# Expert stage of a two-layer decoder: order of weight loads, halves of two weights, and the place of the last scatters

## The chip, the cores and the metric

The kernel runs on one NeuronCore of one Trainium2 chip. Its engines work side by side, each from an in-order queue of its own: TensorE (PE; its weight loads are shown apart as PEld), VectorE (DVE), ScalarE (ACT), GpSimd (POOL) and SyncE (SP), which issues the DMA transfers here. The metric is the device time of one execution, in microseconds; the kernel is run several times and the median counts.

## What is computed

Two layers of a decoder trunk over 256 tokens of width 1024. Each layer is a mixer (sparse and block-sparse attention in layer 0, stick-breaking attention in layer 1), a LayerNorm, a hierarchical mixture of experts (16 experts, hidden width 256), and another LayerNorm. The change lies in the mixture of experts:

```python
def hierarchical_moe(x, w_grp, b_grp, w_rt, b_rt, w_gate, w_up, w_down):
    p_grp = jax.nn.softmax((x @ w_grp + b_grp).astype(jnp.float32), axis=-1)
    g = jnp.argmax(p_grp, axis=-1)
    ...
    top_val, top_idx = lax.top_k(logits, TOPK_IN_GROUP)
    w_e = jax.nn.softmax(top_val, axis=-1) * w_g[..., None]
    expert_id = g[..., None] * EXPERTS_PER_GROUP + top_idx
    combine = jnp.sum(jax.nn.one_hot(expert_id, N_EXPERTS, dtype=jnp.float32) * w_e[..., None], axis=2)
    def per_sequence(args):
        xs, cs = args
        h = jax.nn.silu(jnp.einsum('sd,edf->sef', xs, w_gate)) * jnp.einsum('sd,edf->sef', xs, w_up)
        return jnp.einsum('sef,efd->sd', h * cs[..., None].astype(h.dtype), w_down)

for layer in range(DEPTH):
    x = layer_norm(DEEPNORM_ALPHA * x + mix, ln_mix_g[layer], ln_mix_b[layer])
    ffn = hierarchical_moe(x, ...)
    x = layer_norm(DEEPNORM_ALPHA * x + ffn, ln_ffn_g[layer], ln_ffn_b[layer])
```

Each token uses two experts, so the kernel computes only the rows that are routed, with all 16 experts' weights read once per layer.

## The kernel before

`trunk` runs mixer, expert stage, mixer, expert stage. The expert stage (`moe_`, L1040 to L1453) treats the experts in seven **units** (`POS`, L1030): units 0 to 3 are pairs of experts with 64 slots each, unit 4 (`OV`) takes the tokens over an expert's slots, units 5 and 6 are four experts each with 32 slots. Experts 0 to 5 (units 0 to 2) stand at fixed places; the others are sorted by their load on the chip, so that the addresses of their weights are read from a table (`eid`, L1191) by SP.

Each unit has the same steps on PE:

- **gather** (L1231): tokens are picked into slots by products with a one-hot matrix.
- **front**, the gate and up products (L1264): over 8 chunks of the width; each expert of a unit works in a strip of the array of its own (`lanes`, `tile_position`), 2 or 4 strips at a time. One such product in the code is two rows of the trace.
- **act_h**: silu on ACT (L1270) and a product on DVE (L1272); then two transposes on PE (L1279) and a copy `hT` on ACT (L1280).
- **down** (L1296): the down products, in the same strips, for two halves of the columns; ACT and DVE split each half of the result into a high and a low part (L190, L198).
- **scatter** (L1305, in the last unit's `scatter_end` L1311): the parts are added into four accumulators (two token tiles by two column halves), 8 products of 512 columns a unit.

The steps of neighbouring units are interleaved by hand (L1375 to L1448): front(u+1) stands ahead of down(u), and so on. Within that program order a scheduler of the framework places each instruction on its engine by its own estimate of when operands are there; `tc.issue_after(ins)` forbids it to place an instruction ahead of `ins`.

Weights come through one queue, issued by SP in order. Gate and up weights (`wgu`) go into a ring of six 2 MB buffers (`wtile`, tag `w`), which the mixer's weights share; down weights (`wd`, 1 MB) into four buffers of their own (`wd_tile`), one extra (`wd_extra`) and one place of the ring. A load can be issued once PE has read the last of what stood in its buffer, and a load that waits holds up all behind it on SP. Units 0 and 1 are loaded by `load_gu` (L427): one tile holds chunks 0 to 3 of both experts, the next chunks 4 to 7. Unit 2 is loaded at L1052 to L1058 by whole experts, each in one tile, so that both tiles are read until the end of front(2). Units 5 and 6 are loaded by quarters (`load_gu_of`, L1194): chunks 2j and 2j+1 of four experts, four transfers of 512 KB. In the text wd(2,1) is the down weight of unit 2's second expert, and down(5), front(2) a unit's step.

At the end of the stage `out_tile` adds the residual and does the LayerNorm: between the layers `mid` (L1529), which also transposes the result into `xT` (L309, copies L316 on ACT) for the next mixer's first projection (L254); at the end of the program `fin` (L1559).

Of the kernel before, what the change touches and what calls it, by code (L numbers as in the profile page):

```python
# [17 lines left out]
S, D, NT, NCH = 256, 1024, 2, 8  # L18
# [15 lines left out]
def trunk(ctx, tc, io):  # L34
# [10 lines left out]
    last = {}  # L45
# [23 lines left out]
    def chunks(w):  # L69
        return w.rearrange("p (c n) -> p c n", c=NCH)  # L70
# [969 lines left out]
    def moe_(pm, wk, l, x, lg, xhl, out_tile, before_end):  # L1040
# [9 lines left out]

        wloads[l, 2, 0] = {}
        for i in range(2):  # L1052
            w = chunks(wtile("wgu"))
            SP.dma_start(w, io["wgu"][l * NE + 4 + i])
            for c in range(NCH):
                wloads[l, 2, 0][i, c] = w[:, c]
            if i == 0:
                load_d_at(2, 0, wd_extra())  # L1058
# [155 lines left out]


# [43 lines left out]
        def gate_up(u, g):  # L1259
            ws = wloads[l, u, 0]  # L1260
            pg = pmt()
            for c in range(NCH):
                for k, r in lanes(u):
                    PE.matmul(pg[r, :], g[:, c, BASE[u] + r.start:BASE[u] + r.stop], ws[k, c],  # L1264
                              start=(c == 0), stop=(c == NCH - 1), tile_position=(0, r.start))
            return pg
# [23 lines left out]
        def down(u, dst=(None, None)):  # L1290
            ys, hT, wd = [], hs[u], wloads[l, u, 1]
            for h in range(2):
                y = pmt()
                for fc in range(2):
                    for k, r in lanes(u):
                        PE.matmul(y[r, :], hT[:, fc, r], wd[k][:, fc, h * 512:h * 512 + 512],  # L1296
                                  start=(fc == 0), stop=(fc == 1), tile_position=(0, r.start))
                ys.append(split_y(y, dst[h]))
            return ys
# [7 lines left out]
        def scatter_end(u1, u2):  # L1307

            for u, h, t in ((u2, 0, 0), (u1, 0, 1), (u1, 1, 1), (u2, 1, 0), (u2, 0, 1), (u2, 1, 1)):
                for i in range(2):  # L1310
                    last["PE"] = PE.matmul(oacc[t][h], ST[:, u, t * 128:t * 128 + 128], ys[u][h][i], start=False, stop=(u == u2 and i == 1)).ins  # L1311
# [77 lines left out]
        do_down(0)  # L1389
        load_d_at(2, 1, wd_tile())  # L1390
        load_d_of(3, 0, wd_tile())
        load_gu_of(5, 0)
# [43 lines left out]
        load_d_of(6, 3, wd_extra())  # L1436
# [4 lines left out]
        hid[6], _ = act_h(6, pg)  # L1441
        do_tr(6)
        act_set("natural_log_exp_and_others")
        do_scatter(5, [0])
# [3 lines left out]
        scatter_end(5, 6)  # L1448
# [204 lines left out]
```

## Time and profile before

| | |
|---|---|
| median of 3 runs | 533.94 us (533.82 to 534.5) |
| the profiled execution | 533.85 us, of which the span of instructions is 531.9 us |
| expert stage, layer 0 / layer 1 | about 163 to 271 us / 411 to 517 us |
| DMA moved | 150.02 MB, mean 282 GB/s over the span; 317 to 431 GB/s in the stretches of the expert stages |
| granted PE clock | 1.00 from 16 us to the end of the last product |

The profile is one execution. Times in its rows are microseconds from the start of the span; a row of the timeline gives start, duration, engine, line, output and inputs, how many instructions are merged in it, and in brackets the idle time of the engine before it and what ended that idle time. Line numbers are those of the kernel before.

### The profile page before, as it was taken

The page shows a single profiled execution, that of the slowest core. Times are in us where ns is not written, and L with a number is a line of the kernel's source. Part 1 is how long each engine was busy: PE and PEld are TensorE (multiplying, and loading weights), DVE is VectorE, ACT ScalarE, POOL GpSimd, SP SyncE. Part 2 cuts the span into 40 slices and gives each one's busy share as a digit, 9 for nine tenths or more (in the row PEclk, how much of TensorE's full clock was granted, in tenths as well). Part 3 has the DMA queues.
Part 4 walks back from the last instruction along what each step waited for, and adds up shares of the span by engine and source line. Part 5 has one row for each costly group of instructions (what it writes and reads, how often), then busy time and mean ns, then how long its engine had stood idle before and what let it go on. Part 6 is the DMA issues. An engine that isn't in the chain of part 4 may idle for free.

```text
span 531.9 us, 8516 instructions
## 1 busy us (share of the span) xinstructions
PE 501.4 (94%) x3201; PEld 316.4 (59%) x3201; DVE 289.5 (54%) x824; ACT 220.8 (42%) x433; POOL 7.6 (1%) x18
## 2 busy tenths in 40 slices
PE   8899989999999999999899999999999999999980
PEld 6687656676676354543354996898777454363320
DVE  5878796849669621221166555555648861141125
ACT  4545645547556121121144347556747321131022
POOL 1000000000020000000000000000002000000000
PEclk9999999999999999999999999999999999999995
DMA  8999500009938999999997980003976599999952
GB/s 243 381 429 429 217 0 1 1 0 393 412 152 322 415 363 335 421 422 422 432 430 307 370 341 1 0 1 147 427 297 238 224 394 342 402 423 419 427 217 84
DMA packets 25536, 150.02 MB, mean 282 GB/s; under 512 B 3472, under 2 KB 4112, under 8 KB 14992
## 3 DMA queue, kind: packets, MB, share of 16 engines
q1 hardware_dynamic: 25488, 149.41, 70.1%
q8 instruction: 27, 0.44, 0.3%
q14 instruction: 21, 0.17, 0.1%
HBM read 148.35 MB, written 1.05 MB: 281 GB/s over the span
## 4 chain that ended last, share of the span: by engine, by line
PE 82%; DVE 9%; ACT 4%; DMA 2%; issue 1%; SPq 0%; ACTq 0%; DVEq 0%
PE pmt L1264 16%; PE pmt L1296 9%; PE pmt L1231 4%; PE acc L1305 3%; PE acc L246 3%; PE acc L245 3%; PE acc L398 3%; PE acc L244 3%; PE acc L396 3%; PE acc L397 3%; PE acc L254 3%; DMA wb<-w 2%; PE acc L268 2%; PE acc L266 2%; PE acc L267 2%; PE z L880 2%
## 5 line engine op out<-in xcount | busy, mean ns | idle before, releaser
L1264 PE MATMUL pmt<-wgu,xg 128*64 128x512 f32 (+1 forms) x512 | 92.8, 595 | 0.0
L1264 PEld LDWEIGHTS pmt<-wgu,xg 128*64 128x64 f32 (+1 forms) x512 | 27.2, 123 | 52.9 <-issue 50.8
L190 ACT ACTIVATE wh<-wb 128x1024 fp32r<-128x1024 f32 (+2 forms) x44 | 41.1, 944 | 37.4 <-PE acc L267 19.7
L193 DVE TENSOR_TENSOR wl<-wb,wh 128x512 fp32r<-128x512 f32 (+1 forms) x72 | 45.1, 660 | 19.0 <-ACT wh L190 18.9
L1296 PE MATMUL pmt<-wd,hT 128*64 128x512 f32 (+1 forms) x256 | 53.9, 597 | 0.9 <-ACT hT L1280 0.9
L198 DVE TENSOR_TENSOR yl<-pmt,yh 128x512 fp32r<-128x512 f32 x20 | 13.8, 690 | 47.5 <-ACT yh L190 47.5
L246 PE MATMUL acc<-wl,xhl 128*128 128x512 f32 (+1 forms) x96 | 37.7, 395 | 1.5 <-DVE wl L193 1.5
L244 PE MATMUL acc<-wh,xhl 128*128 128x512 f32 (+1 forms) x96 | 37.3, 389 | 1.4 <-ACT wh L190 1.4
L245 PE MATMUL acc<-wh,xhl 128*128 128x512 f32 (+1 forms) x96 | 37.0, 386 | 0.0
L1272 DVE SCALAR_TENSOR_TENSOR hh<-pmt,cs,silu 128x256 f32<-128x256 f32 x12 | 5.8, 484 | 56.8 <-ACT silu L1270 56.8
L1270 ACT ACTIVATE silu<-pmt 128x256 f32<-128x256 f32 x12 | 4.6, 384 | 76.1 <-PE pmt L1264 76.1
L190 ACT ACTIVATE yh<-pmt 128x512 fp32r<-128x512 f32 x20 | 11.9, 597 | 55.9 <-PE pmt L1296 55.9
L1296 PEld LDWEIGHTS pmt<-wd,hT 128*64 128x64 f32 (+1 forms) x256 | 15.3, 123 | 27.0 <-issue 24.9
L1231 PEld LDWEIGHTS pmt<-Poh,xhl 128*128 128x128 f32 x192 | 24.4, 188 | 5.3 <-issue 3.2
L266 PE MATMUL acc<-xhl,wh 128*128 128x256 f32 x96 | 27.5, 287 | 0.0
L1231 PE MATMUL pmt<-Poh,xhl 128*128 128x256 f32 (+1 forms) x192 | 26.7, 292 | 0.3 <-DVE xg L1239 0.3
L268 PE MATMUL acc<-xhl,wl 128*128 128x256 f32 x96 | 26.9, 280 | 0.0
L267 PE MATMUL acc<-xhl,wh 128*128 128x256 f32 x96 | 26.8, 279 | 0.0
L398 PE MATMUL acc<-xol,oT 128*128 128x512 f32 x64 | 26.1, 412 | 0.0
L396 PE MATMUL acc<-xo,oT 128*128 128x512 f32 x64 | 25.9, 410 | 0.0
L397 PE MATMUL acc<-xo,oT 128*128 128x512 f32 x64 | 25.5, 401 | 0.0
L581 ACT ACTIVATE Pm<-pst,nm 128x128 f32<-128x128 f32 (+1 forms) x48 | 19.8, 419 | 10.7 <-DVE nm L579 9.5
(368 smaller groups left out, 984.0 us busy)
## 6 DMA issues: line engine op xcount, KB each, us to landing
wd<-wd SPq DMA_DIRECT2D x34, 1024.0 KB, 11.0
wgu<-wgu SPq DMA_DIRECT2D x64, 512.0 KB, 11.1
wgu<-wgu SPq DMA_DIRECT2D x14, 2048.0 KB, 12.1
wb<-w1s SPq DMA_DIRECT2D x6, 2048.0 KB, 19.1
wo<-wo SPq DMA_DIRECT2D x4, 2048.0 KB, 16.2
wgu<-wgu SPq DMA_DIRECT2D x8, 1024.0 KB, 7.2
wb<-w SPq DMA_DIRECT2D x3, 2048.0 KB, 22.0
wb<-w SPq DMA_DIRECT2D x2, 1024.0 KB, 8.9
```

Source lines behind the costliest of these rows:

```text
L190: A.activation(dst_h, src, AF.Copy)
L193: V.tensor_tensor(dst_l[:, i], src[:, i], dst_h[:, i].bitcast(F32), OP.subtract)
L244: PE.matmul(a[t][:, :n], xh[:, cc, ts], wh[:, c, :n], start=(cc == 0), stop=False)
L245: PE.matmul(a[t][:, :n], xl[:, cc, ts], wh[:, c, :n], start=False, stop=False)
L246: PE.matmul(a[t][:, :n], xh[:, cc, ts], wl[:, c, :n], start=False, stop=(cc == NCH - 1))
L266: PE.matmul(o, wh[:, c, fs], xh[:, cc], start=(cc == 0 and f % 2 == 0), stop=False, skip_group_check=True)
L396: PE.matmul(a[t][h], oc[:, 0, ts], wh[:, hs], start=first, stop=False)
L397: PE.matmul(a[t][h], oc[:, 1, ts], wh[:, hs], start=False, stop=False)
L398: PE.matmul(a[t][h], oc[:, 0, ts], wl[:, hs], start=False, stop=last)
L1231: PE.matmul(p[:, 0:w], src[:, t, c * 128:c * 128 + 128], P[:, t, u * 128:u * 128 + w], start=(t == 0 and src is xh), stop=(t == 1 and src ...
L1264: PE.matmul(pg[r, :], g[:, c, BASE[u] + r.start:BASE[u] + r.stop], ws[k, c], start=(c == 0), stop=(c == NCH - 1), tile_position=(0, r.start))
L1296: PE.matmul(y[r, :], hT[:, fc, r], wd[k][:, fc, h * 512:h * 512 + 512], start=(fc == 0), stop=(fc == 1), tile_position=(0, r.start))
```

## The change

It has four edits, all in the expert stage, for both layers.

1. **Pair 2 by chunk halves.** Unit 2's gate and up weights are loaded by `load_gu(l, 2)` as those of units 0 and 1 are, with wd(2,0) behind both instead of between them.
2. **Order of loads.** The first quarter of unit 5 (`load_gu_of(5, 0)`) goes ahead of wd(2,1) and wd(3,0).
3. **The last down weight**, wd(6,3), is loaded in two transfers of 512 columns each (`load_d_half`).
4. **Scatters.** The scatters of unit 5 may not be placed ahead of the last gate product of unit 6, and those of unit 6 not ahead of its last down product; `scatter_end` takes its six pairs in another order.

```diff
         load_gu(l, 1)
-
-        wloads[l, 2, 0] = {}
-        for i in range(2):
-            w = chunks(wtile("wgu"))
-            SP.dma_start(w, io["wgu"][l * NE + 4 + i])
-            for c in range(NCH):
-                wloads[l, 2, 0][i, c] = w[:, c]
-            if i == 0:
-                load_d_at(2, 0, wd_extra())
+        load_gu(l, 2)
+        load_d_at(2, 0, wd_extra())
...
+        def load_d_half(u, i, wd, h):
+
+            hs = slice(h * 512, h * 512 + 512)
+            SP.dma_start(wd[:, :, hs], io["wd"][l * NE:(l + 1) * NE][ds(expert(POS[u][i]), 1)].rearrange("e p (f n) -> p (e f) n", f=2)[:, :, hs])
+            wloads.setdefault((l, u, 1), {})[i] = wd
...
-                    PE.matmul(pg[r, :], g[:, c, BASE[u] + r.start:BASE[u] + r.stop], ws[k, c],
-                              start=(c == 0), stop=(c == NCH - 1), tile_position=(0, r.start))
+                    last["G"] = PE.matmul(pg[r, :], g[:, c, BASE[u] + r.start:BASE[u] + r.stop], ws[k, c],
+                                          start=(c == 0), stop=(c == NCH - 1), tile_position=(0, r.start)).ins
...
-        def scatter_end(u1, u2):
-
-            for u, h, t in ((u2, 0, 0), (u1, 0, 1), (u1, 1, 1), (u2, 1, 0), (u2, 0, 1), (u2, 1, 1)):
-                for i in range(2):
-                    last["PE"] = PE.matmul(oacc[t][h], ST[:, u, t * 128:t * 128 + 128], ys[u][h][i], start=False, stop=(u == u2 and i == 1)).ins
+        def scatter_end(u1, u2, down2):
+
+            for u, h, t in ((u1, 0, 1), (u1, 1, 1), (u2, 0, 0), (u2, 1, 0), (u2, 0, 1), (u2, 1, 1)):
+                with (tc.issue_after(down2) if u == u2 else nullcontext()):
+                    for i in range(2):
+                        last["PE"] = PE.matmul(oacc[t][h], ST[:, u, t * 128:t * 128 + 128], ys[u][h][i], start=False, stop=(u == u2 and i == 1)).ins
...
         do_down(0)
+        load_gu_of(5, 0)
         load_d_at(2, 1, wd_tile())
         load_d_of(3, 0, wd_tile())
-        load_gu_of(5, 0)
...
-        load_d_of(6, 3, wd_extra())
+        w63 = wd_extra()
+        for h in range(2):
+            load_d_half(6, 3, w63, h)
...
         pg = front(6)
         hid[6], _ = act_h(6, pg)
+        gate6 = last["G"]
         do_tr(6)
         act_set("natural_log_exp_and_others")
-        do_scatter(5, [0])
+        with tc.issue_after(gate6):
+            do_scatter(5, [0])
...
-        scatter_end(5, 6)
+        with tc.issue_after(gate6):
+            scatter_end(5, 6, last["D"])
```

The order of instructions on the engines changes at few places. On PE, at the end of the expert stage (layer 0's rows; layer 1's are alike), from the last down product of unit 5 on, before. `wgu_2581` and `wgu_2586` are the last two quarters of unit 6's gate and up weights, `yh` and `yl` the two parts of unit 5's result, `x8` eight products in a row:

```order
L1264 MATMUL pmt_2673<-wgu_2581,xg_2499 32x512
L1305 MATMUL acc_1878<-yh_2649,ST_1877 128x512
L1305 MATMUL acc_1878<-yl_2650,ST_1877 128x512
L1264 MATMUL pmt_2673<-wgu_2581,xg_2499 32x512
L1305 MATMUL acc_1879<-yh_2662,ST_1877 128x512
L1305 MATMUL acc_1879<-yl_2663,ST_1877 128x512
L1311 MATMUL acc_1880<-yh_2649,ST_1877 128x512
L1311 MATMUL acc_1880<-yl_2650,ST_1877 128x512
L1311 MATMUL acc_1881<-yh_2662,ST_1877 128x512
L1311 MATMUL acc_1881<-yl_2663,ST_1877 128x512
L1264 MATMUL pmt_2673<-wgu_2581,xg_2499 32x512 x6
L1264 MATMUL pmt_2673<-wgu_2586,xg_2499 32x512 x8
```

And in the changed kernel, from the same place on, where L1263, L1304 and L1278 are the lines of gate products, scatters and transposes:

```order
L1263 MATMUL pmt_2674<-wgu_2581,xg_2499 32x512 x8
L1263 MATMUL pmt_2674<-wgu_2586,xg_2499 32x512 x8
L1304 MATMUL acc_1878<-yh_2649,ST_1877 128x512
L1304 MATMUL acc_1878<-yl_2650,ST_1877 128x512
L1304 MATMUL acc_1879<-yh_2662,ST_1877 128x512
L1304 MATMUL acc_1879<-yl_2663,ST_1877 128x512
L1311 MATMUL acc_1880<-yh_2649,ST_1877 128x512
L1278 MATMUL pmt_2712<-identf_79,hh_2709 128x128 x2
L1311 MATMUL acc_1880<-yl_2650,ST_1877 128x512
L1311 MATMUL acc_1881<-yh_2662,ST_1877 128x512
L1311 MATMUL acc_1881<-yl_2663,ST_1877 128x512
```

The sixteen gate products stand together, five scatters stand between them and the transposes, and three between the transposes and unit 6's down products, which follow in both kernels in the same order. Ahead of these rows the order of PE is unchanged.

On SP, in the middle of layer 0's expert stage (layer 1's is alike), before. `wgu_2082` is the overflow unit's weight, `wgu_2134` the first quarter of unit 5, `wd_2130` and `wd_2132` are wd(2,1) and wd(3,0), and TENSOR_LOAD and ISA fetch an expert's number:

```order
L1207 DMA wgu_2082<-wgu 128x4096
L1045 DMA wd_2130<-wd 128x2048
L1212 ISA
L1212 DMA wd_2132<-wd 128x2048
L1191 TENSOR_LOAD eid_1872
L1191 ISA x2
L1200 ISA
L1200 DMA wgu_2134<-wgu 128x1024
```

In the changed kernel the four transfers of that quarter (now `wgu_2130`) follow the overflow unit's directly; the rows from the last of them on, with L1184, L1193 and L1205 for the lines L1191, L1200 and L1212 of before, and `wgu_2241` as the second quarter of unit 5:

```order
L1184 TENSOR_LOAD eid_1872
L1184 ISA x2
L1193 ISA
L1193 DMA wgu_2130<-wgu 128x1024
L1045 DMA wd_2171<-wd 128x2048
L1205 ISA
L1205 DMA wd_2173<-wd 128x2048
L1193 ISA
L1193 DMA wgu_2241<-wgu 128x1024
```

The two down weights have moved behind all of the quarter.

On ACT one instruction moves, between the layers, in the LayerNorm behind layer 0's expert stage. `lnst_2757` is the statistics tile of the first token tile, `lnst_2828` that of the second; L316 copies the first tile's transposed result. Before:

```order
L353 ACTIVATE acc_1878,lnst_2757<-xn_127,lnst_2757 128x512
L353 ACTIVATE acc_1879,lnst_2757<-xn_127,lnst_2757 128x512
L356 ACTIVATE lnst_2757<-lnst_2757 128x1
L357 ACTIVATE lnst_2757<-lnst_2757 128x1
L316 ACTIVATE xT_2756<-pmt_2806 128x4x128
L316 ACTIVATE xT_2756<-pmt_2813 128x4x128
L353 ACTIVATE acc_1880,lnst_2828<-xn_127,lnst_2828 128x512
L353 ACTIVATE acc_1881,lnst_2828<-xn_127,lnst_2828 128x512
```

In the changed kernel (the statistics tiles are 2758 and 2829 there):

```order
L353 ACTIVATE acc_1878,lnst_2758<-xn_127,lnst_2758 128x512
L353 ACTIVATE acc_1879,lnst_2758<-xn_127,lnst_2758 128x512
L356 ACTIVATE lnst_2758<-lnst_2758 128x1
L357 ACTIVATE lnst_2758<-lnst_2758 128x1
L353 ACTIVATE acc_1880,lnst_2829<-xn_127,lnst_2829 128x512
L316 ACTIVATE xT_2757<-pmt_2807 128x4x128
L316 ACTIVATE xT_2757<-pmt_2814 128x4x128
L353 ACTIVATE acc_1881,lnst_2829<-xn_127,lnst_2829 128x512
```

The first Square of the second tile stands ahead of both copies of the first. DVE's and GpSimd's orders are the same in both kernels.

More of the change, by code (lines that the diff above doesn't have):

```diff
@@ L1295, in down @@
                     for k, r in lanes(u):
-                        PE.matmul(y[r, :], hT[:, fc, r], wd[k][:, fc, h * 512:h * 512 + 512],
-                                  start=(fc == 0), stop=(fc == 1), tile_position=(0, r.start))
+                        last["D"] = PE.matmul(y[r, :], hT[:, fc, r], wd[k][:, fc, h * 512:h * 512 + 512],
+                                              start=(fc == 0), stop=(fc == 1), tile_position=(0, r.start)).ins
                 ys.append(split_y(y, dst[h]))
```

## The prediction

> **What bounds the kernel now.** I read the page first, then TensorE's (PE's) timeline at the end of each layer's expert stage, then the waits for weights and the DMA queue, and last the stretch between the layers.
>
> ```profile
> span 531.9 us, 8516 instructions
> PE 501.4 (94%) x3201; PEld 316.4 (59%) x3201; DVE 289.5 (54%) x824; ACT 220.8 (42%) x433; POOL 7.6 (1%) x18
> PE 82%; DVE 9%; ACT 4%; DMA 2%; issue 1%; SPq 0%; ACTq 0%; DVEq 0%
> ```
>
> PE is busy for 94% of the span and carries 82% of the chain that ended last, so a microsecond counts only where PE is freed. "Busy" can hide loss, though: an expert product (L1264, L1296) fills only a strip of the array, and two or four strips run side by side only while the queue offers products for all of them. The end of layer 1's expert stage shows it (start, duration, line, products, number of them, idle before):
>
> ```profile
> 500.77 1.05 PE L1296 MATMUL pmt<-wd,hT 128*32 128x512 f32 x4
> 501.75 0.50 PE L1305 MATMUL acc<-yh,ST 128*128 128x512 f32 x1
> 502.79 1.04 PE L1264 MATMUL pmt<-wgu,xg 128*32 128x512 f32 x2
> 503.77 0.51 PE L1305 MATMUL acc<-yh,ST 128*128 128x512 f32 x1
> 505.04 0.40 PE L1311 MATMUL acc<-yl,ST 128*128 128x512 f32 x1
> 505.37 3.63 PE L1264 MATMUL pmt<-wgu,xg 128*32 128x512 f32 x28
> 510.00 0.44 PE L1279 MATMUL pmt<-identf,hh 128*128 128x128 f32 x2 [1.00 <-DVE hh L1272]
> 510.91 4.47 PE L1296 MATMUL pmt<-wd,hT 128*32 128x512 f32 x32 [0.47 <-ACT hT L1280]
> ```
>
> Down products of unit 5 end; eight scatters follow from 501.75, with two lone gate products in one strip between them; the last 28 gate products of unit 6 run only at 505.37. Then PE idles 1.00 us for silu and hh and 0.47 us for hT, with no work left to put there. Layer 0 ends with the same rows 245.6 us earlier, but for the last:
>
> ```profile
> 264.43 0.44 PE L1279 MATMUL pmt<-identf,hh 128*128 128x128 f32 x2 [1.00 <-DVE hh L1272]
> 265.34 3.68 PE L1296 MATMUL pmt<-wd,hT 128*32 128x512 f32 x32 [0.47 <-ACT hT L1280]
> ```
>
> There the last down products take 3.68 us, in layer 1 4.47. The waits of PE's weight loads in layer 1 name the cause:
>
> ```profile
> PEld pmt L1264 <- DMA wgu<-wgu: 0.3, 1, 0.3
> PEld pmt L1296 <- DMA wd<-wd: 0.2, 1, 0.2
> ```
>
> One wait for wd, and one other for weights in the whole expert stage. The program's last down weight was issued at 501.04 and landed 10.7 us later, at 511.7 (SP's row, then the row of DMA issues of that moment: number, size, us to landing):
>
> ```profile
> 501.04 0.33 SPq L1212 DMA_DIRECT2D wd<-wd  x1
> wd<-wd SPq DMA_DIRECT2D x1, 1024.0 KB, 10.7
> ```
>
> **Part 1: queue order and pair 2 by chunk halves.** SP's queue in layer 1, and PE's pieces that release its buffers:
>
> ```profile
> 423.24 7.04 PE pmt L1264 x32
> 431.49 3.58 PE pmt L1296 x16
> 462.42 3.58 PE pmt L1296 x16
> 426.87 0.33 SPq L1207 DMA_DIRECT2D wgu<-wgu  x1
> 435.09 0.34 SPq L1045 DMA_DIRECT2D wd<-wd  x1
> 446.54 4.74 SPq L1200 DMA_DIRECT2D wgu<-wgu  x8
> 434.00:456.00 22.00, 22.00 (x118) 11.12 (x116) 6.19 (x12) 4.88 (x9) 0.00 (x0) 1.00 0.95 347
> 456.00:500.00 44.00, 42.67 (x333) 20.28 (x333) 9.86 (x24) 7.70 (x17) 0.00 (x0) 1.00 1.02 418
> ```
>
> After 426.87 SP stands on wd(2,1) until down(0) ends at 435.07, although the buffer of unit 5's first weights is free when front(1) ends at 423.24 + 7.04 = 430.28. Then the next eight weight loads go only at 446.54, when front(2) releases both tiles of pair 2 together. The two windows (last column GB/s) price these holes: 347 against 418 GB/s over 22 us is 22 x (1 - 347/418) = 3.7 us of queue. Now unit 5's first loads go at 430.3, and the first half tile of pair 2 is free halfway through front(2), 3.5 us sooner. I take the whole stream behind as up to 3.7 us earlier. **In itself that is worth nothing**: PE hardly waits for weights. It is the cover of parts 2 and 3. wd(2,1) and wd(3,0), now behind, land some 4 us later; down(2), which reads the first of them, starts at 462.42, over 25 us after its issue. In layer 0, pair 2's second tile no longer stands behind a wd that waits; nobody waits for that tile either.
>
> **Part 2: scatters behind the gate products.** After the last two slots of down(5) (500.77, 501.20; 0.43 us apart) the gate products follow at 501.63 instead of 505.37. The four strips need as long as before, 3.63 us, since three of them still have eight products to come: the end moves from 509.00 to 505.26, and with the same 1.00 us for silu and hh the transposes could go at 506.26. Five scatters stand ahead of them: the first starts 0.55 us behind the last gate start (502.79 + 0.43 to 503.77), 505.21, and six starts took 503.77 to 505.04, so PE is free at 506.48. Transposes 0.44, then three scatters of 0.23 and 0.33 us to the next strip product (505.04 to 505.37): down(6) starts at 507.70, not 510.91. **3.2 us in each layer**: the scatters now cover the two idle gaps, and the gates run four strips wide at once. ACT and DVE have no other work at that place.
>
> **Part 3: the last weight by column halves.** ACT's copies of the two output halves, layer 0 then layer 1:
>
> ```profile
> 268.25 0.60 ACT L190 ACTIVATE yb<-pmt 128x512 fp32r<-128x512 f32 x1 [1.66 <-PE pmt L1296]
> 269.07 0.60 ACT L190 ACTIVATE yb<-pmt 128x512 fp32r<-128x512 f32 x1 [0.23 <-PE pmt L1296]
> 513.82 0.60 ACT L190 ACTIVATE yb<-pmt 128x512 fp32r<-128x512 f32 x1 [1.66 <-PE pmt L1296]
> 515.41 0.60 ACT L190 ACTIVATE yb<-pmt 128x512 fp32r<-128x512 f32 x1 [1.00 <-PE pmt L1296]
> ```
>
> The second copy comes 3.73 us behind the start of down(6) in layer 0, 4.50 in layer 1: the weight costs 0.77 us now, and with part 2 would cost more. It is still issued at 501.04 (its buffer is released by down(5)). With the queue 3.7 us earlier the whole would land at 508.0 and the first half 1.2 us sooner, 506.8. The floor is 501.04 plus the time to landing in an empty queue:
>
> ```profile
> wgu<-wgu SPq DMA_DIRECT2D x1, 512.0 KB, 4.4
> ```
>
> 505.4. Before, the second copy came 3.70 us behind the landing, so without loss the first half must land by 507.70 + 3.73 - 3.70 = 507.7: 0.9 us of margin. The second half is read four slots later. I take no stall: the second copy at 511.43, **4.0 us earlier in layer 1**; behind it the tail of LayerNorm and stores is unchanged. The added issue (0.33 us of SP) hides behind the transfers already queued: 10.7 us to landing there against the 4.4 us above.
>
> The Trainium skill, page "DMA: Bandwidth & Descriptors", section "Bandwidth", says to batch DMAs to 1 MiB or more for 75% of peak; by that rule the halves, at 512 KB, would move at under 0.75 x 418 = 314 GB/s, the first land 0.4 us later by estimate and the margin shrink to 0.5 us, while the sum stayed. The row above 456:500 speaks against it: that window moved mostly 512 KB pieces, at 418 GB/s.
>
> **Part 4: what the scheduler did on the side.** The order shows one change on ACT: between the layers, the Square of the second row tile (L353) now stands ahead of the two copies that give the first tile's xT (L316).
>
> ```profile
> 276.62 1.13 ACT L316 ACTIVATE xT<-pmt 128x512 f32<-128x512 f32 x2 [2.31 <-PE pmt L309]
> 277.28 7.13 PE L254 MATMUL acc<-wb,xT 128*128 128x512 f32 x16 [0.15 <-ACT xT L316]
> 277.60 0.21 DVE L346 TENSOR_SCALAR lnst<-lnst 128x1 f32<-128x1 f32 x1
> 277.85 0.69 ACT L353 ACTIVATE acc<-xn,lnst 128x512 f32<-128x512 f32 x1
> 278.57 0.67 ACT L353 ACTIVATE acc<-xn,lnst 128x512 f32<-128x512 f32 x1
> 285.53 7.13 PE L254 MATMUL acc<-wb,xT 128*128 128x512 f32 x16 [0.25 <-ACT xT L316]
> ```
>
> L353 needs the mean from L346, so it cannot start before 277.85, and the copies, ready at 276.62, stand behind it until 278.57, when the next ACT instruction starts now. PE's projection starts 0.66 us behind the copy: **1.95 us lost**, at a place where PE has nothing else; bounds are 0, if another chain turns out to hold PE there, and 2.1, with the accumulator read of L353 as well. The second tile's chain slips by about 1.1 us but had more slack than that.
>
> **The sum.** Layer 0: -3.21 + 1.95 = -1.26. Layer 1: -3.21 - 0.77 = -3.98. Together -5.24. The profiled execution took 533.85 us (span 531.9 and 1.95 around it), so 528.61; the median of the runs is 0.09 above it: **528.7 us**.
>
> **Rivals.** (a) *The weight becomes the bound.* If the queue gains nothing, the first half lands at 511.7 - 1.2 = 510.5 instead of by 507.7: 2.7 us lost in layer 1; in layer 0 (same stream, landing about 1.3 us earlier against the stage's end) some 0.5. That gives 531.9; half the gain, 2 us, leaves 0.9 and 529.6. For it: the tiles released late stay late. Against: both holes are waits that the new order removes. 0.13 for a loss over 1 us.
>
> (b) *The hand-over costs nothing*: 526.7. For it: PE is behind elsewhere in the mixer too. Against: PE's row follows the copy at 0.15 us. 0.12.
>
> (c) *Slower: gate weights late.* The gate products now stand ahead of the scatters in an in-order queue, so a late weight holds both. The last lane of unit 6's gate weights was issued and landed so:
>
> ```profile
> 491.41 0.33 SPq L1200 DMA_DIRECT2D wgu<-wgu  x1
> wgu<-wgu SPq DMA_DIRECT2D x1, 512.0 KB, 9.8
> ```
>
> 501.2, against first use of that tile four slots behind 501.63, 503.4. Each microsecond behind that costs one per layer. To eat 5.24 us it must land 2.6 us behind, at 506.0, 4.8 later than before; at 507.2 the time would be 528.7 + 2 x 3.8 = 536.3. The stream moves the other way, so 0.04.
>
> (d) *PE's clock.* The hand-over pause of PE grows to about 2.1 us.
>
> ```profile
> 490.00:492.00 2.00, 0.93 (x8) 0.49 (x4) 1.13 (x2) 0.87 (x2) 0.00 (x0) 1.00 1.02 420
> ```
>
> The granted clock (the last figure but two) stayed 1.00 through a pause of 1.07 us. If 2.1 us halved it for half of the 7.13 us projection, it would cost 3.6 us: 532.3. The Trainium skill, page "TensorE: Matmul & The Clock Gate", section "Part 1: The HAM clock gate", puts the fall at an idle window of about 3.4 us; by that rule 2.1 us keeps the clock, and the trace so far agrees as far as 1.07 us goes. 0.03.
>
> (e) *The change doesn't do what it says*: the gate strips do not run four wide behind down(5), or the scatters cost more among transposes; half of part 2 is gone, 531.9, or nearly all of the gain. 0.08.
>
> **How the numbers follow.** The forecast, 528.0 to 529.5, has 0.60; (a) 0.13, (b) 0.12, (c) 0.04, (d) 0.03, (e) 0.08. The range reaches from (b) to (a) at its worst: 526.4 to 531.9. A change of under about 0.2% (1.07 us) cannot be told from none. Faster by more holds the forecast, (b), nearly all of (a) and (d) and half of (e): 0.90; within 0.2%: 0.06; slower: 0.04.
>
> **What would show it.** Right: the last 30-odd gate products in one run directly behind unit 5's down products, the idle before L1279 and the last down products nearly gone, both ACT copies about 0.8 us apart in layer 1, the ACT copy of xT about 2 us behind its transposes. Wrong: down products of unit 6 that wait for wd, gate products that wait for wgu, a projection that starts 0.66 us behind the transposes' copy with no wait on L353, or a mixer of layer 1 that shortens by what was lost ahead of it.

## The result, and the profile after

The changed kernel takes **529.33 us** (median of 13 runs) against 534.12 for the kernel before on the same chip: ratio **0.9919, 95% interval 0.9900 to 0.9938** (computed from the runs; it is not the quotient of the two medians), so it is faster by 0.6 to 1.0%. Twelve of the runs lie between 527.53 and 533.25 us; one took 703.32 us at a mean granted PE clock of 0.65 and does not enter the ratio. The prediction was 528.7. The profiled execution took 529.95 us, its span 528.2. First the page: span, TensorE (PE) and the chain of work that ended last.

```profile
span 528.2 us, 8526 instructions
...
PE 81%; DVE 9%; DMA 5%; ACT 3%; issue 1%; SPq 0%; ACTq 0%; DVEq 0%
```

DMA has gone from 2% to 5% of the chain: something now waits for a transfer. The end of layer 1's expert stage on PE (start, duration, line, products, number of them):

```profile
501.62 0.62 PE L1295 MATMUL pmt<-wd,hT 128*32 128x512 f32 x2
501.69 3.99 PE L1263 MATMUL pmt<-wgu,xg 128*32 128x512 f32 x27
505.61 0.51 PE L1304 MATMUL acc<-yh,ST 128*128 128x512 f32 x1
...
506.89 0.38 PE L1278 MATMUL pmt<-identf,hh 128*128 128x128 f32 x2
...
507.58 0.40 PE L1311 MATMUL acc<-yl,ST 128*128 128x512 f32 x1
507.90 3.90 PE L1295 MATMUL pmt<-wd,hT 128*32 128x512 f32 x32
```

The gate products run in one piece behind unit 5's down products, and neither the transposes nor the last down products have an idle time before them any more. The down products start at 507.90, where 507.70 was forecast. They take 3.90 us: still a little over the 3.68 of an undisturbed stage. ScalarE's two copies of the result, and SP's row of the two halves of the last weight, which is 1.34 us from the first issue's start to the second's end, where the whole weight took 0.33:

```profile
510.81 0.60 ACT L190 ACTIVATE yb<-pmt 128x512 fp32r<-128x512 f32 x1 [1.82 <-PE pmt L1295]
511.85 0.60 ACT L190 ACTIVATE yb<-pmt 128x512 fp32r<-128x512 f32 x1 [0.44 <-PE pmt L1295]
...
501.46 1.34 SPq L1211 DMA_DIRECT2D wd<-wd  x2
```

The DMA issues of those two moments (number, size, us to landing):

```profile
wd<-wd SPq DMA_DIRECT2D x1, 512.0 KB, 6.7
wd<-wd SPq DMA_DIRECT2D x1, 512.0 KB, 7.2
```

The first half landed at 501.46 + 6.7 = 508.2 (forecast 506.8), 0.5 us over the 507.7 that it needed, and the second copy came at 511.85 (forecast 511.43). Layer 0 holds what was not foreseen. PE, then VectorE (DVE), then ACT at its end and the hand-over to layer 1 (the stretch between layer 0's last scatters and the first projection of layer 1's mixer):

```profile
246.49 2.77 PE L1295 MATMUL pmt<-wd,hT 128*32 128x512 f32 x3
...
262.65 3.68 PE L1295 MATMUL pmt<-wd,hT 128*32 128x512 f32 x32
...
274.48 1.13 PE L309 MATMUL pmt<-identf,xn 128*128 128x128 f32 x8
277.68 7.13 PE L254 MATMUL acc<-wb,xT 128*128 128x512 f32 x16 [2.07 <-ACT xT L316]
...
268.64 0.69 DVE L344 SCALAR_TENSOR_TENSOR xn<-xn,acc 128x512 f32<-128x512 f32 x1 [0.33 <-PE acc L1311]
...
269.37 0.21 DVE L346 TENSOR_SCALAR lnst<-lnst 128x1 f32<-128x1 f32 x1
270.66 1.28 DVE L372 SCALAR_TENSOR_TENSOR lnu<-xn,lnst,lngb 128x1024 f32<-128x1024 f32 x1 [1.08 <-DMA lngb<-lng]
...
276.33 0.69 ACT L353 ACTIVATE acc<-xn,lnst 128x512 f32<-128x512 f32 x1 [3.53 <-DVE lnst L346]
277.05 1.06 ACT L316 ACTIVATE xT<-pmt 128x512 f32<-128x512 f32 x2
```

Three idle times have come in: PE waits 2.07 us for the copies of xT, as forecast; VectorE waits 1.08 us for a LayerNorm row (`lngb`), which is new and was not forecast, and 0.33 us for a scatter. And three products near 246.5 took 2.77 us. Before, the same three products took 1.48, and VectorE did not wait for the row:

```profile
247.38 1.48 PE L1296 MATMUL pmt<-wd,hT 128*32 128x512 f32 x3
...
272.07 1.28 DVE L372 SCALAR_TENSOR_TENSOR lnu<-xn,lnst,lngb 128x1024 f32<-128x1024 f32 x1
```

The windows of the changed kernel there show why those products took longer (PE busy and its products, PE's loads, VectorE, ScalarE, GpSimd; then granted PE clock, DMA share and GB/s), beside those of the queue in layer 1:

```profile
240.00:244.00 4.00, 4.00 (x27) 1.78 (x25) 0.93 (x5) 0.27 (x1) 0.00 (x0) 1.00 1.03 421
244.00:248.00 4.00, 2.93 (x7) 0.95 (x7) 1.38 (x2) 0.60 (x2) 0.00 (x0) 0.81 1.03 420
248.00:252.00 4.00, 4.00 (x25) 1.15 (x27) 0.00 (x0) 0.00 (x0) 0.00 (x0) 0.76 1.02 430
...
434.00:456.00 22.00, 22.00 (x118) 11.12 (x116) 6.19 (x12) 5.33 (x10) 0.00 (x0) 1.00 1.00 397
456.00:500.00 44.00, 42.67 (x331) 20.25 (x330) 9.86 (x24) 7.70 (x17) 0.00 (x0) 1.00 1.02 419
```

The clock is below 1.00 around 246 to 250; inside the program's work the trace's record of it has one stretch at 0.5, from 246.47 to 249.88.

To compare all runs below, I cut each trace at five instructions. **A** runs from layer 0's first product with the overflow unit's sum `yo` (L1354) to VectorE's first sum (L344): end of the stage, layer 0. **B** runs from there to the second token tile's projection (the second row of 16 products, L254): the hand-over. **C** runs from layer 1's first yo product to its last 32 down products, **D** from there to VectorE's last instruction. What lies between B and C, the whole mixer, was 206.04 to 206.15 us in every trace, so nothing gained or lost in layer 0 was given back there. A star marks a part with a stretch at half clock in it, which costs 1.6 to 1.7 us. (In four traces, act, old_order, no_halves and no_queue, half clock also stood for 3.41 or 6.83 us near 65 us, ahead of all four parts.)

| kernel | A | B | C | D |
|---|---|---|---|---|
| before | 24.32 | 15.23 | 19.33 | 15.29 |
| changed (again: second row) | 22.52* | 18.32 | 15.90 | 14.85 |
| again | 22.53* | 19.61* | 15.89 | 14.98 |
| act | 22.73* | 16.55 | 17.57* | 14.85 |
| act_rows | 20.86 | 15.45 | 15.90 | 14.85 |
| halves_last | 22.52* | 15.21 | 15.88 | 14.86 |
| warm | 20.86 | 15.22 | 15.89 | 14.86 |
| old_order | 20.86 | 16.14 | 17.56* | 14.85 |
| no_halves | 22.53* | 15.22 | 15.89 | 15.52 |
| no_queue | 23.13* | 17.80* | 15.89 | 17.28 |
| no_scatter | 25.98* | 15.45 | 19.34 | 14.86 |
| queue_alone | 24.31 | 15.23 | 19.32 | 14.62 |
| halves_alone | 24.30 | 17.37 | 21.00* | 14.85 |
| scatter_alone | 22.97* | 15.11 | 15.90 | 19.58 |

Without stars (A is 20.86 in the kernels of the new order that have none there, which is 22.52 less 1.66) the changed kernel gains 24.32 - 20.86 = 3.46 in A, loses 3.09 in B, gains 3.43 in C and 0.44 in D: 4.24 us, where 5.24 was forecast. In the profiled execution the half clock took 1.66 of it, and its expert stage began 0.89 earlier for reasons ahead of the change.

### The profile page after: what moved, and what is told of

Its sections match the earlier page's. It is cut to its first block, busy times and chain, and to the rows that moved or that the text cites. A ratio compares the mean times of both kernels' runs of the same rounds, so it can differ in the third digit from the quotient of the medians.

```text
span 528.2 us, 8526 instructions
## 1 busy us (share of the span) xinstructions
PE 498.5 (94%) x3201; PEld 318.0 (60%) x3201; DVE 289.4 (55%) x824; ACT 220.5 (42%) x433; POOL 7.6 (1%) x18
## 4 chain that ended last, share of the span: by engine, by line
PE 81%; DVE 9%; DMA 5%; ACT 3%; issue 1%; SPq 0%; ACTq 0%; DVEq 0%
PE pmt L1263 16%; PE pmt L1295 8%; PE pmt L1230 5%; PE acc L1304 3%; PE acc L246 3%; PE acc L245 3%; PE acc L398 3%; PE acc L244 3%; PE acc L396 3%; PE acc L397 3%; PE acc L254 3%; DMA lngb<-lng 2%; DMA wb<-w 2%; PE acc L268 2%; PE acc L266 2%; PE acc L267 2%
## 5 line engine op out<-in xcount | busy, mean ns | idle before, releaser
L1263 PE MATMUL pmt<-wgu,xg 128*64 128x512 f32 (+1 forms) x512 | 92.8, 599 | 0.0
L1263 PEld LDWEIGHTS pmt<-wgu,xg 128*64 128x64 f32 (+1 forms) x512 | 28.6, 124 | 53.8 <-issue 52.7
L1295 PE MATMUL pmt<-wd,hT 128*64 128x512 f32 (+1 forms) x256 | 55.0, 604 | 0.0
```

Of the source, the lines that this page charges most:

```text
L1263: last["G"] = PE.matmul(pg[r, :], g[:, c, BASE[u] + r.start:BASE[u] + r.stop], ws[k, c], start=(c == 0), stop=(c == NCH - 1), tile_positio ...
L1295: last["D"] = PE.matmul(y[r, :], hT[:, fc, r], wd[k][:, fc, h * 512:h * 512 + 512], start=(fc == 0), stop=(fc == 1), tile_position=(0, r.s ...
```

## Experiments

Each ran beside the kernel before, in five rounds. The ratio to that kernel is given with its 95% interval in brackets; that kernel's medians were 534.2 to 534.8. The kernels have only 5 to 12 runs each, and half clock moves a run by 1.7 us at a time, so differences of under about 2 us between two experiments are read from the parts A to D, not from the medians.

**The changed kernel again** (`again`, no edit).

> The changed kernel as it is, once more. In its first profile the granted clock stood at 0.5 for one stretch of 3.41 us (246.37 to 249.78) inside the gate products of layer 0, where before had 1.00, and that cost 1.66 us. Theory (the stretch comes by chance, not from the new order): in a new profile it lies elsewhere or is missing, and the mean granted clock of the runs wanders between 0.98 and 0.99 as it did; median 529.3, fastest near 527.5. Rival (the new order of products makes it): the profile shows half clock again between 245 and 251, and all runs lie within 0.5 us of 529.9.

Measured: 531.06 us, 0.9935 (0.9911 to 0.9959). Half clock came at 246.73 again, so the theory missed; but also at 277.45, in PE's 2.08 us pause for xT, and the runs spread from 529.25 to 532.68, so the rival missed as well. What decides comes with `warm`.

**ScalarE's order held** (`act`): the Squares of the second tile wait for the copies.

```diff
-        with tc.issue_after(last["u"]):
+        with tc.issue_after(last["u"]), (tc.issue_after(last["X"]) if t and pin else nullcontext()):
             rs = ln_rstd(r, accs, st)
...
-            ln_tile(t, x[:, t], a, gb, u, done, 0 if t else 30)
+            ln_tile(t, x[:, t], a, gb, u, done, 0 if t else 30, True)
```

`last["X"]` is the copy of xT in `transp4`; the last line sets `pin`, in `mid` alone. All kernels below have this edit, except `queue_alone` and `halves_alone`.

> The changed kernel with the two Squares of the second token tile (L353) held behind the two copies of the first tile's xT (L316) on ScalarE, at the layer hand-over, as they stood before the change. Theory (the side effect costs what the drift of the two traces says): TensorE's wait ahead of the first block of 16 products (L254, 2.07 us for the copy) goes back to about 0.2, the second one to about 1; 1.84 us go, ratio 0.9885 where the changed kernel has 0.9919, some 527.5 us. Rival (the hand-over is bound by the second tile's row statistics anyway): the time stays at 529.3 and TensorE waits as long for the second tile's copies.

Measured: 526.91 us, 0.9863 (0.9838 to 0.9889). PE and VectorE at the hand-over:

```profile
277.09 7.13 PE L254 MATMUL acc<-wb,xT 128*128 128x512 f32 x16 [0.15 <-ACT xT L316]
...
271.99 1.28 DVE L372 SCALAR_TENSOR_TENSOR lnu<-xn,lnst,lngb 128x1024 f32<-128x1024 f32 x1 [1.42 <-DMA lngb<-lng]
```

PE's wait is back at 0.15 and B is 1.77 shorter, although the wait for the row has grown by 0.34. (In this trace the first sum of layer 0 comes 0.2 us later and the second does not wait for its scatter, so 0.2 us lie in A that lie in B elsewhere.) With both corrections the side effect cost 1.77 + 0.34 - 0.20 = 1.91, what its term said; the rival falls.

**LayerNorm rows first** (`act_rows`).

```diff
-        if before_end:
-            before_end(-1)
         gb = load_ln(2 * l + 1, wk.tile([128, 2, D], F32, name="lngb", tag="Poh"))
+        if before_end:
+            before_end(-1)
```

> As the one before, and the two LayerNorm rows of the layer's end are requested ahead of the 2 MB block of the next layer's weights instead of behind it. Theory: VectorE's wait of 1.08 us for the row (landing 270.56, behind a block that landed 269.35) goes, since the row lands some 4.9 us earlier, near 265.7; another 1.04 us go, ratio 0.9866, some 526.5 us. The block lands 2.5 us later, near 271.9, and is first needed after 275, so it costs nothing. Rival (VectorE is not the chain there, or the block becomes late): no gain over the one before, or a wait of TensorE for wb at L254.

Measured: 525.91 us, 0.9853 (0.9826 to 0.9880). The row's issue on SP and VectorE's two instructions, then the DMA issue with its time to landing:

```profile
256.43 0.53 SPq L332 DMA_DIRECT2D lngb<-lng  x1
...
267.28 0.69 DVE L344 SCALAR_TENSOR_TENSOR xn<-xn,acc 128x512 f32<-128x512 f32 x1 [0.33 <-PE acc L1311]
...
268.26 1.28 DVE L372 SCALAR_TENSOR_TENSOR lnu<-xn,lnst,lngb 128x1024 f32<-128x1024 f32 x1
```

```profile
lngb<-lng SPq DMA_DIRECT2D x1, 512.0 KB, 8.0
```

The row lands at 264.4, the wait is gone, and B falls from 16.55 to 15.45; PE does not wait for the block that comes later. 0.24 over before's B stays: the 0.33 us ahead of the second sum, where the last scatters stand regrouped, the product with a half's low part directly behind the one with its high part.

**No column halves** (`no_halves`).

```diff
-        w63 = wd_extra()
-        for h in range(2):
-            load_d_half(6, 3, w63, h)
+        load_d_of(6, 3, wd_extra())
```

> The changed kernel with ScalarE's order held as in act, and the very last down weight loaded whole (1 MB) again. Theory (halves let the first column half of the products start one half transfer, 1.36 us by the landings 508.14 and 509.50, earlier): in layer 1 the products wait in the first column half until about 509.5, the second copy of the result comes about 1.3 us later than in act, and the time is 1.2 to 1.4 us above act; nothing changes in layer 0, where the weight has time. Rival (the queue order alone brings the weight in time): the same time as act within 0.3 us.

Measured: 529.39 us, 0.9897 (0.9870 to 0.9924). D is 0.67 longer, not 1.2 to 1.4, and the down products take 4.70 us:

```profile
506.88 4.70 PE L1295 MATMUL pmt<-wd,hT 128*32 128x512 f32 x32
```

Right in sign, half the size. Layer 0, which I had expected unchanged, is shorter: B stands at 15.22 where act has 16.55. The wait for the LayerNorm row is gone, although the row still stands behind the 2 MB block. SP's rows of the last weight of layer 0 and of the LayerNorm row in act, then the same in no_halves with VectorE's instruction:

```profile
257.20 1.45 SPq L1211 DMA_DIRECT2D wd<-wd  x2
259.40 0.36 SPq L332 DMA_DIRECT2D lngb<-lng  x1
```

```profile
258.26 0.33 SPq L1205 DMA_DIRECT2D wd<-wd  x1
259.18 0.37 SPq L332 DMA_DIRECT2D lngb<-lng  x1
271.41 1.28 DVE L372 SCALAR_TENSOR_TENSOR lnu<-xn,lnst,lngb 128x1024 f32<-128x1024 f32 x1
```

With halves the row is issued 2.20 us behind the weight, with the weight whole 0.92 us behind it. By the parts without stars this kernel is 6.7 us under before, 0.9 less than act; its median is 2.5 us over act's, which the parts do not show, and I did not find out why.

**Old queue order** (`no_queue`): edits 1 and 2 undone; pair 2 by whole experts with the lines removed by the change, and

```diff
-        load_gu_of(5, 0)
         load_d_at(2, 1, wd_tile())
         load_d_of(3, 0, wd_tile())
+        load_gu_of(5, 0)
```

> The changed kernel with ScalarE's order held as in act, and the old order of the queue: pair 2 by whole weights with the down weight between, and the loads of pair 5 behind two waiting down weights. Theory (the order's only worth is that the end of layer 1's stream lands 2.0 to 2.4 us earlier, by 499.28 against 501.22 and 506.80 against 509.20): the last halves land near 510.3 and 511.7 and bound layer 1, 2.0 to 2.6 us above act; layer 0 unchanged, since its last weight is not waited for. Rival (the stream catches up, since the last weight is issued only when its buffer is free): within 0.3 us of act.

Measured: 531.65 us, 0.9950 (0.9932 to 0.9968). The last down products of layer 1:

```profile
509.01 6.47 PE L1302 MATMUL pmt<-wd,hT 128*32 128x512 f32 x32
```

D is 17.28, 2.43 over act, inside the forecast. Layer 0 was not quite unchanged: its last weight, too, held the down products, and A without its star is some 0.6 us longer. A and B each hold a half-clock stretch.

**Old places of the scatters** (`no_scatter`): edit 4 undone, with the old order in `scatter_end`, and

```diff
-        with tc.issue_after(gate6):
-            do_scatter(5, [0])
+        do_scatter(5, [0])
```

> The changed kernel with ScalarE's order held as in act, and the scatters where they were before the change (spread among the gate products), with queue order and halves kept. Theory: down(6) starts 3.0 to 3.5 us later in each layer, what is left is the gain on the last weight of layer 1, 0.5 to 0.8 us against before: 533.4, ratio 0.9985 to 0.999. The wait for the LayerNorm row in layer 0 is gone, since VectorE comes 3 us later. Rival (queue order and halves carry a part of the layer gain of their own): ratio under 0.996.

Measured: 534.05 us, 0.9987 (0.9969 to 1.0006). C is 19.34 as before, A without its star too, and D is 14.86: without the moved scatters the gain of A and C is gone.

**The scatters alone** (`scatter_alone`): the kernel before with edit 4 of the change and ScalarE's order held.

> The kernel before with the scatters moved behind the gate products alone (no queue order, no halves; ScalarE's order as before). Theory: layer 0 gains 2.2 to 3.2 us (3.46 less 0.23 for the order of the scatters, less up to 1 for the LayerNorm row), layer 1 gains nothing, because the last down weight, landing near 511.7 less what layer 0 gained, bounds it as it did: 531 to 532, ratio 0.994 to 0.996. Rival (layer 1 is bound by the order of the products, not the weight): layer 1 gains its 3 us too, ratio 0.989.

Measured: 533.77 us, 0.9989 (0.9968 to 1.0009), under the forecast gain. C falls by 3.43, and D rises by 4.29:

```profile
505.19 2.09 PE L1302 MATMUL pmt<-wd,hT 128*32 128x512 f32 x8
507.84 1.90 PE L1302 MATMUL pmt<-wd,hT 128*32 128x512 f32 x4 [0.55 <-DMA wd<-wd]
510.33 3.62 PE L1302 MATMUL pmt<-wd,hT 128*32 128x512 f32 x20 [0.59 <-DMA wd<-wd]
```

The down products start early and then stand for two weights, the last landing at 510.3. My forecast let layer 1 lose only its own gain, but PE waits 0.86 us longer than that, since layer 0's 3.0 us (A without its star) bring it to the weights early. Without the star the parts add up to a gain of 2.3 us, as forecast; the profile with its star has 0.6, and the runs have at most 1.7 (the interval). What takes the rest of the 2.3 in the runs I did not show. VectorE does not wait for the LayerNorm row here either.

**Old order of the last scatter pairs** (`old_order`).

```diff
-            for u, h, t in ((u1, 0, 1), (u1, 1, 1), (u2, 0, 0), (u2, 1, 0), (u2, 0, 1), (u2, 1, 1)):
-                with (tc.issue_after(down2) if u == u2 else nullcontext()):
+            for u, h, t in ((u2, 0, 0), (u1, 0, 1), (u1, 1, 1), (u2, 1, 0), (u2, 0, 1), (u2, 1, 1)):
+                with nullcontext():
```

So this edit also takes away the hold of unit 6's scatters behind its last down product.

> The changed kernel with ScalarE's order held as in act, and the last six pairs of scatters in their order of before (the first tile's left half first). Theory: in the changed order the low part of a half stands right behind its high part, and waits for VectorE's subtraction while a ready scatter is queued behind; the old order is worth 0.1 to 0.3 us in layer 0 and about 0 in layer 1. Rival: the order changes nothing (within 0.1 in the stretch from the first copy to the first sum).

Measured: 528.11 us, 0.9885 (0.9855 to 0.9915). The rival holds: VectorE's wait of 0.33 ahead of the second sum is there as in the changed kernel, and B is 0.41 under act's with nothing for the order to explain: the wait for the row is shorter (0.82 for 1.42), less the 0.2 that lie in A in act. The order in the code is not what PE's queue got; the next kernel shows what is.

**The halves alone** (`halves_alone`): the kernel before with `load_d_half` only.

> The kernel before with the very last down weight by column halves and nothing else of the change. The order of its instructions has ScalarE's Squares of the second token tile ahead of the copies of xT, and the first two pairs of the last scatters grouped as high and low part, just as the changed kernel has them. Theory (both side effects of layer 0 come from the halves, not from the scatters): layer 0 loses 1.84 (copies) and 0.24 (VectorE waits 0.33 for the second sum's scatter), layer 1 gains 0.4 to 0.8; in all 1.3 to 1.7 us slower than before, ratio 1.002 to 1.004. Rival (the halves are worth in layer 1 what they cost, or ScalarE's order costs nothing where the scatters stand as before): within 0.3 us of before.

Measured: 538.21 us, **1.0067** (1.0042 to 1.0092). By itself this part makes the kernel slower. VectorE, then PE:

```profile
270.50 0.69 DVE L344 SCALAR_TENSOR_TENSOR xn<-xn,acc 128x512 f32<-128x512 f32 x1 [0.33 <-PE acc L1318]
...
278.60 7.13 PE L254 MATMUL acc<-wb,xT 128*128 128x512 f32 x16 [2.07 <-ACT xT L316]
```

Both side effects of layer 0 are there, to 0.01 us, with no scatter moved: B +2.14, D -0.44, 1.7 us without the star, as expected. The runs lost 3.4 (interval 2.2 to 4.9); a star in C covers the rest in the profile, and I did not show that it does in the median.

**The queue order alone** (`queue_alone`): the kernel before with edits 1 and 2 of the change.

> The kernel before with the new order of the queue alone (pair 2 by chunk halves, pair 5's loads ahead of the waiting down weights); last weight whole, scatters and ScalarE's order as before. Theory: the last down weight of layer 1 lands some 17.9 us after the first yo product where before had 20.13 (511.71 less 491.58), and is no longer waited for behind 19.3; from the first down product to the end 14.85 us where before had 15.28, so 0.4 us faster and nothing in layer 0: ratio 0.998 to 1.000, which the runs can hardly tell. Rival (the queue order costs something of its own in the earlier pairs, since pair 2's weight comes in two transfers and its products interleave): the stretch from the first gate product to the first yo product grows, in layer 0 from 65.73 or in layer 1 by over 0.3, and the time is slower by as much.

Measured: 533.03 us, 0.9978 (0.9959 to 0.9996). A, B and C are as before; D is 14.62, 0.67 shorter, and the down products take 3.68 us:

```profile
510.50 3.68 PE L1295 MATMUL pmt<-wd,hT 128*32 128x512 f32 x32 [0.47 <-ACT hT L1279]
```

All of the weight's stall goes by the order alone. The rival falls: from the first gate product to the first yo product it took 78.50 us for 78.48 in layer 0, and 75.96 for 75.96 in layer 1. D is also 0.23 under the 14.85 of the kernels with halves: there the last scatters are regrouped, and VectorE waits 0.33 us ahead of the second sum of layer 1 (in act, no_scatter and halves_alone), which it does not do here.

**Halves in layer 1 only** (`halves_last`, on act_rows).

```diff
+        if l:
             w63 = wd_extra()
             for h in range(2):
                 load_d_half(6, 3, w63, h)
+        else:
+            load_d_of(6, 3, wd_extra())
```

> As act_rows, with the column halves in layer 1 alone (layer 0 loads the last weight whole). Theory: layer 0 loses its wait of 0.33 us between the first two sums (0.24 of it on the path) and keeps 15.12 to 15.21 us from the first sum to the second block of matrix products, where act_rows has 15.45; layer 1 as in act_rows (14.86 us from the first down product to the end). Some 0.2 us under act_rows, ratio 0.985. Rival (layer 0 needs the halves too): the whole weight lands late and its products wait in layer 0, 0.5 to 0.8 us over act_rows.

Measured: 526.69 us, 0.9846 (0.9813 to 0.9879). B is 15.21 and the second sum's wait is gone; the whole weight is in time in layer 0. The 0.24 us show in the trace, not in the runs, which a half clock (A) moves by more.

**PE's wait for yo filled** (`warm`, on halves_last).

```diff
         do_tr(5)
+        with tc.issue_after(last["H"]):
+            keep_warm(8, pmt)
         do_scatter(4)
```

> As halves_last, with 8 products of ones (128x256 bf16, some 0.115 us each) on TensorE in its wait of 1.07 us for the overflow expert's sum (yo, L1354), in both layers; their result isn't used. Theory (TensorE's clock is judged in stretches of 3.41 us whose phase differs from run to run, and a stretch that holds this wait is too idle): in the ten traces so far, 20 such places, half clock followed exactly where a stretch began 1.28 to 2.30 us after the first yo product (9 of 20 places) and never elsewhere there; with the wait filled it follows nowhere, at no cost, and the runs lose the ones that stood 1.7 us (or 3.4) above the fastest: median at most 525.3, at most one run in five over 526.5. Rival (the products with half the rows make the stretch idle, not the wait): half clock still follows in about a third of the runs at each place, spread as before. Rival (the filling delays the yo products): the stretch from the last transposes to the first down product grows by some 0.1 to 0.5 us in each layer.

Measured: 526.06 us, 0.9834 (0.9803 to 0.9864); six runs from 525.07 to 526.11, where halves_last has 525.31 to 528.09. The share of runs held (none of six over 526.5), the median of at most 525.3 did not. PE's timeline at the yo product and the windows there (PE busy and its products, granted clock, DMA share, GB/s) in halves_last, then the same two views of warm:

```profile
244.73 1.46 PE L1354 MATMUL acc<-yo,ST 64*128 64x512 f32 x4 [1.07 <-DVE yo L1347]
246.11 2.35 PE L1295 MATMUL pmt<-wd,hT 128*32 128x512 f32 x3
```

```profile
246.00:248.00 2.00, 2.00 (x7) 0.64 1.05 436
248.00:250.00 2.00, 2.00 (x12) 0.51 1.00 422
```

```profile
244.47 1.04 PE L327 MATMUL pmt<-oneb 128*128 128x256 bf16 x8
245.71 1.46 PE L1354 MATMUL acc<-yo,ST 64*128 64x512 f32 x4 [0.19 <-DVE yo L1347]
247.09 1.48 PE L1295 MATMUL pmt<-wd,hT 128*32 128x512 f32 x3
```

```profile
246.00:248.00 2.00, 2.00 (x10) 1.00 1.04 426
248.00:250.00 2.00, 2.00 (x17) 1.00 1.02 430
```

A and C are at their best values, so the filling delays nothing. This is the best version found: 8.8 us under before, some 1.7% against the change's 0.6 to 0.8%.

## Why the prediction was near, by its steps

- **Part 1, queue order: the direction held, both sizes were off.** The text took the stream 3.7 us earlier. The window 434 to 456 moved 397 GB/s for 347, which by the same sum is 22 x (397 - 347)/418 = 2.6 us, and the last gate weight landed 1.9 us earlier, at 489.46 + 9.8 = 499.3 for 501.2 (SP's row, then the DMA issue):

```profile
489.46 0.33 SPq L1193 DMA_DIRECT2D wgu<-wgu  x1
```

```profile
wgu<-wgu SPq DMA_DIRECT2D x1, 512.0 KB, 9.8
```

"In itself that is worth nothing" was wrong by 0.67 us: `queue_alone` shows that the order alone takes the whole of D's stall, the same stall that part 3 booked for the halves. As cover it was needed: `no_queue` is rival (a) made real, and it lost 2.43 us in D and 0.6 in A against the 2.7 and 0.5 of the text. (For the 0.5 the text let layer 0's last weight land about 1.3 us earlier against the end of its stage; by the rows it landed at 255.46 + 8.5 = 264.0, which is 2.2 us earlier, and the 0.5 fits that.)
- **Part 2, scatters: right, a little small.** 3.21 forecast in each layer, 3.46 and 3.43 measured. With neither queue order nor halves (`scatter_alone`) the gain of C came back whole as a wait for weights.
- **Part 3, halves: right for layer 1 in mechanism, not in size, and wrong for layer 0.** 0.77 was forecast in layer 1, 0.44 measured. D without any stall is 14.62 (`queue_alone`), 0.67 under before, and the regrouped scatters take 0.23 back. That the first half landed at 508.2, not 506.8, cost no more: act's last down products took 3.68 us, without a stall, and its D is the same 14.85. The halves are worth 0.67 there once the scatters are moved (no_halves against act). That the added issue, 0.33 us of SP, hides did not hold: the two halves took 1.45 us of SP in layer 0, and the LayerNorm row was issued 1.3 us later behind the weight than without them (2.20 for 0.92, act and no_halves).
- **Part 4, the side effect: right.** 1.95 forecast, 1.91 measured: from PE's transposes to its projection 277.68 - 274.48 = 3.20 us, before 277.28 - 275.99 = 1.29 (row below); rival (b) falls, since the mixer behind it kept its length. The text called it what the scheduler did on the side and named no edit: it is the halves (`halves_alone`).

```profile
275.99 1.13 PE L309 MATMUL pmt<-identf,xn 128*128 128x128 f32 x8
```

- **What the sum lacked**, both in layer 0: the LayerNorm row (270.66 - 269.37 = 1.29 us from L346 to L372 where before had 272.07 - 271.82 = 0.25, so 1.04 on the path), and the regrouped scatters (0.24). With 1.91 that is 3.19; B lost 3.09, since 0.10 of the row's wait is caught up behind it. The text let layer 0 gain the whole of part 2. But VectorE is ready for L372 at 269.6, before at 272.0, and the row, queued behind a 2 MB block, landed at 258.43 + 12.1 = 270.5 where before had it at 256.38 + 13.7 = 270.1. Both the moved scatters and the halves are needed for the wait: with the row behind the block and the scatters moved, VectorE waited 0.68 to 1.56 us in all five kernels with halves in layer 0 (changed, again, act, old_order, no_queue) and not at all in the two with the weight whole (no_halves, scatter_alone). So all of B's loss goes back to edit 3, the row's part of it together with edit 4. The text asked what is late next of the weights only, not of the LayerNorm's own operands.
- **Rival (d), the clock, had 0.03 and came true in two places**, one by its own mechanism: in `again` half clock fell into the 2.08 us pause and cost 1.7 us, not 3.6. The rule of the Trainium skill (page "TensorE: Matmul & The Clock Gate", section "Part 1: The HAM clock gate") that the clock falls after an idle window of some 3.4 us was read as an idle time of that length. The traces differ: 1.07 us of idle time were enough. That the trace of before kept 1.00 through its pauses of 1.07 us was chance, as the last section shows.

With the terms as measured, -3.46 + 3.09 - 3.43 - 0.44 = -4.24 and the median forecast would have been 529.7; 529.33 and 531.06 were measured in the two sets. So the mechanisms of parts 2 and 4 held, but that the first median came within 0.7 us of 528.7, and inside 528.0 to 529.5, is luck in part: the gain forecast too small in part 2 (0.47) hides some of the loss left out in layer 0 (1.14 in B) and of the gain that was not there in part 3 (0.33), and the second set's median lies outside 528.0 to 529.5.

## What to carry to other kernels

When work is taken off the path, follow every operand of the next instructions, small ones too: a 4 KB row that is broadcast behind a 2 MB block is as late as the block, and a weight that goes out in two transfers makes it later still. Test each edit of a bundle alone and look at the order of all engines, since an edit to one transfer regrouped instructions on two engines in another place and cost more than it brought: the halves gave 0.67 us in layer 1 and lost 3.1 in layer 0, where nothing needed them (halves_last). An edit that frees an engine is worth only as much as the next transfer lets it be: by the parts without stars, the moved scatters gained 2.3 us alone (scatter_alone) and 6.7 with the queue order (no_halves), where the order alone gains 0.7.

## What was not expected of the hardware

TensorE's clock fell to half for 3.41 us at places where it idled for only 1.07 us. In each trace these stretches lie on a grid: 246.47 and 516.12 in the changed kernel are 79 x 3.413 us apart. The grid's phase against the program differs from run to run. For every first yo product I took the time to the next grid point. In the 13 traces with the wait unfilled (26 places) half clock began there at 1.28, 1.37, 1.59, 1.69, 1.84, 1.86, 2.17, 2.20, 2.21, 2.27 and 2.30 us, and at none of the others (0.09 to 1.09, ten places; 2.37 to 2.90, five). So it follows when the 3.41 us ahead of a grid point hold the whole wait of 1.07 us and at least the next 1.28 us, in which the yo products, which use half the rows, run for 1.46 us. In before the two places lay at 0.92 and 1.09, just short of the range. The range is about a third of a grid step, in each of two places, and each hit costs 1.66 us: that can make much of the spread of these runs, before and after; the other places with half clock, near 65 us and in the hand-over, I did not look into. With the wait filled, the two places of `warm` lay at 1.84 and 2.01, inside the range, and the clock stayed at 1.00; that is one trace, and the narrow spread of its six runs goes with it. The Trainium skill, page "TensorE: Matmul & The Clock Gate", section "Part 1: The HAM clock gate", has a free-running window of 3413 ns that does not reset when a kernel starts, and the grid agrees with it. How busy a window must be to keep the clock is bounded by these runs for this place only.
